# The latent attention's low rotated keys held in two zero-filled tiles of 128 rows

## The chip, the cores and the metric
One core of one Trainium2 chip runs the whole program. The metric is device time in microseconds (us) from launch to end. The kernel before takes 2837.29 us (median of 3 runs, 2834.54 to 2839.94).

## The reference, cut to what matters
The program is two transformer blocks on 512 tokens of width 1024: gated linear attention and a feed-forward layer, then multi-head latent attention (MLA) and a feed-forward layer, then a second block with convolution and expert lookup. The change lies in the MLA scores alone:

```
q_nope (8 heads x 128), q_rope (8 heads x 64);  k_nope (8 heads x 128), k_rope (64, one for all heads)
q_rope, k_rope = apply_rope(q_rope), apply_rope(k_rope)
s = (q_nope . k_nope  +  q_rope . k_rope) * 192 ** -0.5
p = softmax(where(key <= query, s, -inf));  o = p @ v
```

Everything is float32 in the reference.

## The kernel before
A tensor that enters a large product is kept as two parts in the fp32r format, a high part (the rounded value) and a low part (what rounding left). `split` (L240) makes them: ScalarE (ACT) copies the high part, VectorE (DVE) subtracts it for the low part. A product of two such tensors is three matmuls, high by high, high by low, low by high; `mm3` issues them at L274, L275 and L276. Weights arrive in units of 1 MB (`raw`, two buffers, issued from SyncE's queue, SP, at L267), and each unit is split the same way into `whi` and `wlo`. The engines run in parallel and meet at semaphores; each engine takes its instructions in one fixed order that a planner sets when the program is built.

The MLA stage runs in this order. Projections give the latents; the key's rotary part `pa`, `pb` is rotated on DVE into `kr` (L841 to L845). `kr` holds the same 64 rotated rows twice, on partitions 0 to 63 and 64 to 127. L846 and L847 split it into `krh` and `krl` (both named kr in the profile), each of 128 rows. The values `vn` follow (L857 to L861), and then the loop over 8 heads.

- `queries(h)`: for every second head it projects and rotates the queries of two heads (L872 to L876) and makes for each a tile `qs` (L880 on ACT, L881 on GpSimd, POOL). For an even head the tile has the high rotated query on rows 0 to 63 and the low one on rows 64 to 127; for an odd head it is the other way round. For every head it then projects and splits `kn` and `qn` (L240).
- `weigh(h)`: for each of four query blocks `qb`, with n = 128, 256, 384 and 512 keys, five matmuls add into one PSUM bank (L899 to L903). L900 takes all 128 rows of `qx` against `krh`, which gives high by high plus low by high at once. L901 takes only the 64 rows `rr` that hold the high query, against the same 64 rows of `krl`. Then DVE adds the mask (L904), finds the row maximum (L906, L907), ACT takes the exponential (L909), and DVE normalises (L910, L911).
- `attend(h)`: TensorE (PE) transposes the weights (L922), DVE copies them out (L924), PE multiplies by `vn` (L926), and ACT and DVE split the result into `hh` and `hl` (L928, L929).

The loop is written as weigh(h+1), attend(h), queries(h+2), and the planner interleaves them on PE. PSUM has eight banks, four with the tag "mm" and four with "acc". After the heads come the output projection, and further feed-forward and projection stages built on `mm3`.

The pool `mn` has a tag "araw" with two buffers of 128 x 1024. It streams the adaptive-norm weights through SP's queue at L319 for DVE's dot products at L312, in other stages than this one.

Of the kernel before, what the change touches and what calls it, by code (L numbers as in the profile page):

```python
# [10 lines left out]
F32 = mybir.dt.float32  # L11
F32R = mybir.dt.float32r
# [9 lines left out]
P = 128  # L22
S = 512
D = 1024
# [37 lines left out]
ARAW = 2  # L62
# [131 lines left out]
def block_kernel(ctx, tc, x_in, cs_in, wst, vec, cst, gmask, smask, pos, ada1, ada2, wgate, keys, ust, uex, vex, out):  # L194
    nc = tc.nc
    V, A_, T_, G_, SP = nc.vector, nc.scalar, nc.tensor, nc.gpsimd, nc.sync
# [7 lines left out]
    mn = main.enter_context(tc.tile_pool(name="mn", bufs=1))  # L204
    dr = ctx.enter_context(tc.tile_pool(name="dr", bufs=1, space=DRAM))

    def bank(tag="mm"):
        return ps.tile([P, S], F32, tag=tag, bufs=4, name=tag)
# [30 lines left out]
    def split(hi, lo, src, eng=None):  # L239
        state["split"] = (A_.copy(hi, src), (eng or V).tensor_sub(lo, src, hi.bitcast(F32)))  # L240
# [313 lines left out]
    with tc.tile_pool(name="gla", bufs=1, reuse_waits="tile") as gp:  # L554
# [24 lines left out]
        def gates():  # L579

            az, mz = [], []
            for h in range(GLA_H):
                z = bank("acc")
                T_.matmul(z, wg[:, h * P:(h + 1) * P], glr, start=True, stop=True)
                bg = vc("gla_b_gate", h)
                a = gp.tile([P, S], F32, tag="b", bufs=4, name="az")
                m = gp.tile([P, S], F32, tag="vn", bufs=8, name="mz")
                A_.activation(a, z, AF.Abs, bias=bg)
                V.tensor_scalar(m, z, bg, 0.0, op0=ALU.add, op1=ALU.min)
                az.append(a)  # L590
                mz.append(m)
            for a in az:
                e = A_.activation(a, a, AF.Exp, scale=-1.0)
            with tc.issue_after(e.ins):
                for h in range(GLA_H):
                    n = A_.activation(az[h], az[h], AF.Ln, bias=1.0)
                    V.tensor_sub(mz[h], mz[h], az[h])
                    V.tensor_tensor_scan(az[h], smk, mz[h], 0.0, op0=ALU.mult, op1=ALU.add)
            return az, n
# [102 lines left out]
        bs, n = gates()  # L702
        for what in GLA_ORDER.split():
            kind, h = what[0], int(what[1])
# [105 lines left out]
    with tc.tile_pool(name="mla", bufs=1, reuse_waits="tile") as mp:  # L810
# [13 lines left out]
        def latent_norm(ns, sq, gname, tag):  # L824
            rs = bcast(sq.rsqrt(tag))
            for i, n in enumerate(ns):
                V.scalar_tensor_tensor(cq[n], cq[n], vc(gname, i), rs, op0=ALU.mult, op1=ALU.mult)
                ch[n] = mp.tile([P, S], F32R, name=f"ch{n}")
                cl[n] = mp.tile([P, S], F32R, name=f"cl{n}")
                split(ch[n], cl[n], cq[n])  # L830
# [9 lines left out]
        kr = mp.tile([P, S], F32, tag="qr", bufs=1, name="kr")  # L840
        V.tensor_mul(kr, pa, cosT)  # L841
        pb = proj("mla_w_in", hh, hl)
        t = mn.tile([P, S], F32, tag="tmp", bufs=2, name="tmp")
        V.tensor_mul(t, pb, sinT)
        V.tensor_add(kr, kr, t)  # L845
        krh, krl = [mp.tile([P, S], F32R, name=f"kr{i}") for i in range(2)]  # L846
        split(krh, krl, kr)  # L847
        latent_norm((0, 1, 2), sqq, "mla_g_q", "n")
        cqh, cql = [ch[n] for n in range(3)], [cl[n] for n in range(3)]
        vn = [mp.tile([P, 1024], F32, name=f"mv{c}") for c in range(NT)]  # L850
# [38 lines left out]
        def weigh(h):  # L889

            kn, qn = kq.pop(h)
            qx = qrot.pop(h)
            rr = slice(h % 2 * 64, h % 2 * 64 + 64)
            prs = []
            for qb in range(NT):
                n = (qb + 1) * P
                qs = slice(qb * P, (qb + 1) * P)
                sc = bank("mm")
                T_.matmul(sc[:, :n], qn[0][:, qs], kn[0][:, :n], start=True, stop=False)  # L899
                T_.matmul(sc[:, :n], qx[:, qs], krh[:, :n], start=False, stop=False)  # L900
                T_.matmul(sc[:, :n], qx[rr, qs], krl[rr, :n], start=False, stop=False)  # L901
                T_.matmul(sc[:, :n], qn[1][:, qs], kn[0][:, :n], start=False, stop=False)
                T_.matmul(sc[:, :n], qn[0][:, qs], kn[1][:, :n], start=False, stop=True)  # L903
                V.tensor_add(sc[:, qs], sc[:, qs], cm)  # L904
                mx = mp.tile([P, 4], F32, tag="mx", bufs=4, name="mx")
                V.reduce_max(mx[:, 0:1], sc[:, :n], axis=mybir.AxisListType.X)  # L906
                V.tensor_scalar(mx[:, 1:2], mx[:, 0:1], -scale, None, op0=ALU.mult)  # L907
                pr = mp.tile([P, n], F32, tag=f"pr{qb}", bufs=2, name="pr")
                A_.activation(pr, sc[:, :n], AF.Exp, bias=mx[:, 1:2], scale=scale, accum_out=mx[:, 2:3])  # L909
                V.reciprocal(mx[:, 3:4], mx[:, 2:3])  # L910
                V.tensor_scalar(pr, pr, mx[:, 3:4], None, op0=ALU.mult)  # L911
                prs.append(pr)
            return prs
# [17 lines left out]
        prs = {}  # L931
        queries(0)
        prs[0] = weigh(0)
        queries(1)
        for h in range(MLA_H):
            if h + 1 < MLA_H:
                prs[h + 1] = weigh(h + 1)
            attend(h, prs.pop(h))
            if h + 2 < MLA_H:
                queries(h + 2)  # L940
# [31 lines left out]
    with tc.tile_pool(name="b2", bufs=1, reuse_waits="tile") as bp:  # L972
# [4 lines left out]
        for n in range(4):  # L977
            p = proj("w_in_2", hh, hl)
            t = bp.tile([P, WIDE], F32, tag=f"glu{n}", name="glu")[:, :PADC + S]
# [4 lines left out]
        for n in range(4):  # L984
            p = proj("w_in_2", hh, hl)
            t = mn.tile([P, S], F32, tag="tmp", bufs=2, name="tmp")
# [57 lines left out]
        for n in range(16):  # L1044
            p = proj("w_in_2", hh, hl)
            t = bp.tile([P, S], F32, name=f"sg{n}")
# [9 lines left out]
        for g in range(4):  # L1056
# [3 lines left out]
            t = mn.tile([P, S], F32, tag="tmp", bufs=2, name="tmp")  # L1060
# [15 lines left out]
        for n in range(4):  # L1076
            V.scalar_tensor_tensor(yc[n], yc[n], vc("conv_ln_g_2", n), rs, op0=ALU.mult, op1=ALU.mult)
            t = mn.tile([P, S], F32, tag="tmp", bufs=2, name="tmp")
# [19 lines left out]
    with tc.tile_pool(name="peer", bufs=1, reuse_waits="tile") as pp:  # L1098
# [38 lines left out]
        with tc.tile_pool(name="sel", bufs=1, reuse_waits="tile") as sp:  # L1137
# [179 lines left out]
            for h in range(PH):  # L1317
                qq, ql = [], []
                for half in range(2):
                    p = proj("w_query_2", hh, hl)  # L1320
                    t = sp.tile([P, 3 * P], F32, tag="q", bufs=4, name="q")
# [28 lines left out]
        with tc.tile_pool(name="exp", bufs=1, reuse_waits="tile") as ep:  # L1350
# [81 lines left out]
            for g in range(P // GJ):  # L1432
# [13 lines left out]
                for half in range(2):  # L1446
                    acc = [bank("acc") for _ in range(4)]
                    for j4 in range(GJ // 4):
# [3 lines left out]
                        for j in range(4):  # L1452
                            for dd in range(4):
                                o = j * 512 + dd * P
                                i = j4 * 4 + j
# [3 lines left out]
                    for dd in range(4):  # L1459
                        n = half * 4 + dd  # L1460
# [95 lines left out]
```

## Time and profile before

| | |
|---|---|
| Median of 3 runs | 2837.29 us |
| Profiled execution | 2844.19 us |
| Its span, first to last instruction | 2842.3 us |
| Mean granted TensorE clock | 0.981 of full speed |
| PE busy | 2716.3 us, 96% |
| DVE busy | 2109.8 us, 74% |
| ACT busy | 1070.5 us, 38% |
| POOL busy | 704.0 us, 25% |
| MLA head loop | from about 760 to 866 us in the span |

A row of a timeline gives the start in the span, the duration, the engine, the line, the operation, and the output and inputs; idle time before it stands in square brackets with what ended it. PEld is PE's weight load, which can run beside the matmul before it. Matmul ends are modelled, so the distance from one start to the next is the firmer number.

### The profile page before, as it was taken

The page shows a single profiled execution, that of the slowest core. Times are in us where ns is not written, and L with a number is a line of the kernel's source. Part 1 is how long each engine was busy: PE and PEld are TensorE (multiplying, and loading weights), DVE is VectorE, ACT ScalarE, POOL GpSimd, SP SyncE. Part 2 cuts the span into 40 slices and gives each one's busy share as a digit, 9 for nine tenths or more (in the row PEclk, how much of TensorE's full clock was granted, in tenths as well). Part 3 has the DMA queues.
Part 4 walks back from the last instruction along what each step waited for, and adds up shares of the span by engine and source line. Part 5 has one row for each costly group of instructions (what it writes and reads, how often), then busy time and mean ns, then how long its engine had stood idle before and what let it go on. Part 6 is the DMA issues. An engine that isn't in the chain of part 4 may idle for free. (4 is left out here: it accounts for less than half of the span.)

```text
span 2842.3 us, 38989 instructions
## 1 busy us (share of the span) xinstructions
PE 2716.3 (96%) x14889; PEld 2441.4 (86%) x14889; DVE 2109.8 (74%) x4011; ACT 1070.5 (38%) x1530; POOL 704.0 (25%) x556
## 2 busy tenths in 40 slices
PE   6789998999999999999999999998899999999998
PEld 4677887888778878888888889998899999999998
DVE  8874766435776774337966798888989898988986
ACT  4443322222433322233453336653333333333332
POOL 4541100001011000001521420003545455444550
PEclk9899999999999999999999999999999999999999
DMA  6441477422211674232223236656999998998993
GB/s 267 139 137 62 148 259 256 142 95 88 75 45 60 210 264 148 89 104 76 89 89 104 77 120 214 210 196 241 337 340 359 355 340 328 341 344 320 350 344 131
DMA packets 184363, 560.62 MB, mean 197 GB/s; under 512 B 13248, under 2 KB 66912, under 8 KB 157680
## 3 DMA queue, kind: packets, MB, share of 16 engines
q1 hardware_dynamic: 142352, 407.08, 40.9%
q0 software_dynamic: 41472, 151.01, 14.3%
q8 instruction: 117, 1.92, 0.3%
q14 instruction: 70, 0.57, 0.1%
q10 hardware_dynamic: 352, 0.03, 0.0%
HBM read 527.32 MB, written 30.75 MB: 196 GB/s over the span
## 5 line engine op out<-in xcount | busy, mean ns | idle before, releaser
L240 ACT CAST whi<-raw 128x1024 fp32r<-128x1024 f32 x510 | 535.6, 1051 | 1171.4 <-PE mm L275 689.7
L275 PE MATMUL mm<-hl,whi 128*128 128x512 f32 (+2 forms) x2544 | 899.8, 355 | 8.9 <-DVE hl L426 8.1
L274 PE MATMUL mm<-hh,whi 128*128 128x512 f32 (+2 forms) x2544 | 899.7, 355 | 2.7 <-ACT hh L425 2.0
L276 PE MATMUL mm<-hh,wlo 128*128 128x512 f32 (+2 forms) x2544 | 898.8, 354 | 0.1
L240 DVE TENSOR_TENSOR wlo<-raw,whi 128x1024 fp32r<-128x1024 f32 x472 | 580.2, 1230 | 296.8 <-ACT whi L240 288.0
L275 PEld LDWEIGHTS mm<-hl,whi 128*128 128x128 f32 x2544 | 482.4, 190 | 57.4 <-DVE hl L426 9.8
L274 PEld LDWEIGHTS mm<-hh,whi 128*128 128x128 f32 x2544 | 482.5, 190 | 49.5 <-ACT hh L425 2.6
L276 PEld LDWEIGHTS mm<-hh,wlo 128*128 128x128 f32 x2544 | 482.8, 190 | 48.2 <-issue 1.5
L240 POOL TENSOR_TENSOR wlo<-raw,whi 128x1024 fp32r<-128x1024 f32 x38 | 90.7, 2391 | 908.7 <-ACT whi L240 864.0
L1377 POOL DMA_INDIRECT rows<-vex,eidx x144 | 215.2, 1494 | 214.4 <-DVE y L1391 198.1
L1377 POOL DMA_INDIRECT rows<-uex,eidx x144 | 210.1, 1459 | 214.2 <-DVE rows L1381 164.9
L312 DVE SCALAR_TENSOR_TENSOR araw<-araw,sc 128x1024 f32<-128x1024 f32 x128 | 160.6, 1258 | 98.0 <-DMA araw<-ada 97.4
L1391 DVE SCALAR_TENSOR_TENSOR y<-rows,act,y 128x1024 f32<-128x1024 f32 x142 | 181.7, 1280 | 7.3 <-DMA rows<-vex,eidx 6.7
L1381 DVE SCALAR_TENSOR_TENSOR rows<-rows,hn 128x1024 f32<-128x1024 f32 x144 | 170.1, 1220 | 14.8 <-DMA rows<-uex,eidx 14.8
L274 PE MATMUL mm<-fh,whi 128*128 128x512 f32 (+1 forms) x396 | 147.5, 372 | 11.3 <-ACT fh L240 11.3
L275 PE MATMUL mm<-fl,whi 128*128 128x512 f32 (+1 forms) x396 | 147.7, 373 | 1.7 <-DVE fl L240 1.7
L276 PE MATMUL mm<-fh,wlo 128*128 128x512 f32 (+1 forms) x396 | 146.9, 371 | 0.0
L1310 ACT ACTIVATE stage<-acc 128x512 f32<-128x512 f32 x92 | 91.6, 1105 | 37.0 <-PE acc L1307 26.6
L1307 PE MATMUL acc<-oa,ob 128*128 128x128 f16 x736 | 101.5, 296 | 0.3 <-DVE oa L1298 0.2
L274 PEld LDWEIGHTS mm<-fh,whi 128*128 128x128 f32 x396 | 76.2, 192 | 24.6 <-ACT fh L240 12.1
L448 DVE SCALAR_TENSOR_TENSOR x<-mm,mod,x 128x512 f32<-128x512 f32 (+1 forms) x66 | 43.9, 666 | 62.8 <-PE mm L276 62.7
L275 PEld LDWEIGHTS mm<-fl,whi 128*128 128x128 f32 x396 | 76.1, 192 | 15.3 <-DVE fl L240 2.7
(1381 smaller groups left out, 4593.9 us busy)
## 6 DMA issues: line engine op xcount, KB each, us to landing
raw<-wst SPq DMA_DIRECT2D x127, 1024.0 KB, 4.9
araw<-ada SPq DMA_DIRECT2D x128, 512.0 KB, 4.6
raw<-ust SPq DMA_DIRECT2D x64, 1024.0 KB, 6.4
raw<-vex SPq DMA_DIRECT2D x64, 1024.0 KB, 7.6
gd<-stage SPq DMA_DIRECT2D x23, 1024.0 KB, 4.5
gt<-gd SPq DMA_DIRECT2D x16, 1472.0 KB, 9.4
aw<-ada SPq DMA_DIRECT2D x16, 512.0 KB, 8.9
spilled<-a SPq DMA_DIRECT2D x24, 184.0 KB, 3.1
```

The costliest lines, as they stand in the source:

```text
L240: state["split"] = (A_.copy(hi, src), (eng or V).tensor_sub(lo, src, hi.bitcast(F32)))
L274: T_.matmul(out_, wh, ah, start=first, stop=False)
L275: T_.matmul(out_, wh, al, start=False, stop=False)
L276: state["mm"] = T_.matmul(out_, wl, ah, start=False, stop=last)
L312: op(out=w, in0=w, scalar=1.0, in1=sc, op0=ALU.mult, op1=ALU.mult, accum_out=out_)
L448: V.scalar_tensor_tensor(x[n][:, cs], p[:, cs], gate[:, n:n + 1], x[n][:, cs], op0=ALU.mult, op1=ALU.add)
L1307: T_.matmul(p[:, t * P:(t + 1) * P], ob[:, q, :, t], oa[i][:, q, :, t], start=i == 0, stop=i == 1)
L1310: A_.mul(st[:, :, t1:t1 + 4].rearrange("p j t -> p t j"), p.rearrange("p (t j) -> p t j", t=4), 1.0 / GSC)
L1377: G_.indirect_dma_start(out=r, out_offset=None, in_=uex if up_ else vex, in_offset=bass.IndirectOffsetOnAxis(ap=eidx[:, n:n + 1] if n < P ...
L1381: V.scalar_tensor_tensor(r, r, 1.0, hn if n < P else hx, op0=ALU.mult, op1=ALU.mult, accum_out=act[:, n:n + 1])
L1391: V.scalar_tensor_tensor(z, r, act[:, n:n + 1], z, op0=ALU.mult, op1=ALU.add)
```

## The change
`krh` stays as it was. `krl` becomes the two halves of one tile `kz` of 128 x 1024 from the tag "araw". The first half holds the low key on rows 0 to 63 and zeros on rows 64 to 127, the second half the other way round. Two POOL memsets write the zeros, and two DVE subtractions on 64 rows each take the place of one on 128 rows. In `weigh`, the third matmul takes all 128 rows of `qx` against the half that belongs to the head's parity; the rows with the low query meet zeros.

```
-        krh, krl = [mp.tile([P, S], F32R, name=f"kr{i}") for i in range(2)]
-        split(krh, krl, kr)
+        krh = mp.tile([P, S], F32R, name="krh")
+        A_.copy(krh, kr)
+        kz = mn.tile([P, D], F32R, tag="araw", bufs=ARAW, name="kz")
+        krl = kz[:, :S], kz[:, S:]
+        for i, t in enumerate(krl):
+            on, off = slice(i * 64, i * 64 + 64), slice(64 - i * 64, 128 - i * 64)
+            G_.memset(t[off].bitcast(F32), 0.0)
+            V.tensor_sub(t[on], kr[on], krh[on].bitcast(F32))
...
-            rr = slice(h % 2 * 64, h % 2 * 64 + 64)
...
-                T_.matmul(sc[:, :n], qx[rr, qs], krl[rr, :n], start=False, stop=False)
+                T_.matmul(sc[:, :n], qx[:, qs], krl[h % 2][:, :n], start=False, stop=False)
```

## Rows read from the trace of the kernel before

**Rows 1.** The page's busy time, share and count of each engine, and its line of PE's busy tenths in 40 equal slices of the span.
```profile
PE 2716.3 (96%) x14889; PEld 2441.4 (86%) x14889; DVE 2109.8 (74%) x4011; ACT 1070.5 (38%) x1530; POOL 704.0 (25%) x556
PE   6789998999999999999999999998899999999998
```

**Rows 2.** Busy time by stretch: the head loop and a stretch of the expert stage, the longest. Columns: stretch, its length, then busy us (and instructions) of PE, PEld, DVE, ACT and POOL, granted clock, DMA share, GB/s.
```profile
760.00:866.00 106.00, 102.00 (x519) 78.88 (x518) 77.33 (x218) 42.75 (x98) 12.17 (x8) 0.97 0.12 40
...
2100.00:2200.00 100.00, 100.00 (x602) 100.00 (x601) 91.57 (x141) 37.99 (x54) 52.31 (x36) 1.00 0.96 353
```

**Rows 3.** Who waited for whom from 780 to 866 us: total us, times, longest us.
```profile
PEld acc L926 <- DVE pT L924: 4.5, 6, 0.7
...
PEld mm L901 <- issue: 2.9, 9, 0.4
PEld mm L902 <- issue: 2.6, 12, 0.2
PE acc L926 <- DVE pT L924: 2.3, 6, 0.4
```

**Rows 4.** PE's timeline in `weigh(4)`: the first matmul, the groups of 384 and 512 keys, and the transpose that follows.
```profile
819.36 0.33 PE L899 MATMUL mm<-kn,qn 128*128 128x128 f32 x1
...
821.31 0.34 PE L899 MATMUL mm<-kn,qn 128*128 128x384 f32 x1
821.48 0.34 PE L900 MATMUL mm<-kr,qs 128*128 128x384 f32 x1
821.75 0.44 PE L901 MATMUL mm<-kr,qs 64*128 64x384 f32 x1
822.12 0.44 PE L902 MATMUL mm<-kn,qn 128*128 128x384 f32 x1
822.39 0.34 PE L903 MATMUL mm<-kn,qn 128*128 128x384 f32 x1
822.57 0.39 PE L899 MATMUL mm<-kn,qn 128*128 128x512 f32 x1
822.80 0.40 PE L900 MATMUL mm<-kr,qs 128*128 128x512 f32 x1
823.13 0.49 PE L901 MATMUL mm<-kr,qs 64*128 64x512 f32 x1
823.55 0.50 PE L902 MATMUL mm<-kn,qn 128*128 128x512 f32 x1
823.88 0.39 PE L903 MATMUL mm<-kn,qn 128*128 128x512 f32 x1
824.12 1.03 PE L922 MATMUL acc<-ct,pr 128*128 128x128 f32 x8
```

**Rows 5.** PE's weight loads for three of those matmuls of 512 keys.
```profile
822.57 0.19 PEld L900 LDWEIGHTS mm<-kr,qs 128*128 128x128 f32 x1
823.12 0.18 PEld L901 LDWEIGHTS mm<-kr,qs 64*128 64x128 f32 x1 [0.36 <-issue]
823.55 0.19 PEld L902 LDWEIGHTS mm<-kn,qn 128*128 128x128 f32 x1 [0.24 <-issue]
```

**Rows 6.** PE's timeline: 14 matmuls of 128 columns in a row, and the start of the next.
```profile
827.29 1.72 PE L926 MATMUL acc<-pT,mv 128*128 128x128 f32 x14
828.77 0.48 PE L276 MATMUL mm<-ch,wlo 128*128 128x512 f32 x1
```

**Rows 7.** PE's timeline after `weigh(1)`: the start of `attend(0)`'s last products.
```profile
782.63 1.05 PE L926 MATMUL acc<-pT,mv 128*128 128x128 f32 x8
```

**Rows 8.** DVE's timeline after `weigh(1)`: the mask of the last score, and the copy that the products of rows 7 read; last, the first masks of `weigh(4)`.
```profile
779.77 0.30 DVE L904 TENSOR_TENSOR mm<-mm,ct 128x128 f32<-128x128 f32 x1 [0.60 <-PE mm L903]
...
781.31 0.68 DVE L924 COPY pT<-acc 128x512 f32<-128x512 f32 x1
...
821.22 0.59 DVE L904 TENSOR_TENSOR mm<-mm,ct 128x128 f32<-128x128 f32 x2 [1.08 <-PE mm L903]
```

**Rows 9.** PE's timeline at head 0: the first matmul of `weigh(0)`, and the first after its last.
```profile
762.11 0.33 PE L899 MATMUL mm<-kn,qn 128*128 128x128 f32 x1 [1.19 <-ACT qn L240]
...
769.54 0.63 PE L274 MATMUL mm<-ch,whi 128*128 128x512 f32 x1
```

**Rows 10.** Two stretches around the end of `weigh(0)`, with the columns of rows 2; the granted clock is the third number from the end.
```profile
764.00:769.50 5.50, 5.50 (x14) 3.49 (x14) 2.23 (x9) 1.69 (x6) 0.00 (x0) 0.50 0.22 91
...
770.50:771.00 0.50, 0.50 (x4) 0.40 (x3) 0.50 (x4) 0.00 (x0) 0.00 (x0) 1.00 0.00 0
```

**Rows 11.** DVE's timeline: the subtraction that makes `krl`, and the next idle time on DVE.
```profile
745.90 0.68 DVE L240 TENSOR_TENSOR kr<-kr,kr 128x512 fp32r<-128x512 f32 x1
...
748.71 1.23 DVE L240 TENSOR_TENSOR wlo<-raw,whi 128x1024 fp32r<-128x1024 f32 x1 [0.86 <-ACT whi L240]
```

**Rows 12.** POOL's timeline: its first work in the MLA stage, with the idle time before it.
```profile
760.46 3.06 POOL L881 TENSOR_TENSOR qs<-qr,qs 64x512 fp32r<-64x512 f32 x2 [63.25 <-ACT qs L880]
```

**Rows 13.** POOL's memsets of 128 x 512 in an earlier stage: count, then busy us, mean ns of one, idle us before.
```profile
L615 POOL MEMSET at<- 128x512 f32 x4 | 2.0, 529 | 1.1 <-DVE az L598 1.1
```

**Rows 14.** The buffers "araw": DVE's dot products from 100 to 760 us, with the least, median and largest duration in ns and the first and last start.
```profile
L312 DVE SCALAR_TENSOR_TENSOR araw<-araw,sc x76: 1202/1225/1672, 104.2 to 505.4; 128x1024 f32<-128x1024 f32 x76
```

**Rows 15.** SP's timeline: the first loads into "araw" after those.
```profile
940.16 1.47 SPq L319 DMA_DIRECT2D araw<-ada  x2
```

**Rows 16.** All matmuls of L901, with the columns of rows 14.
```profile
L901 PE MATMUL mm<-kr,qs x32: 322/434/792, 762.5 to 864.4; 64*128 64x128 f32 x8, 64*128 64x256 f32 x8, 64*128 64x384 f32 x8, 64*128 64x512 f32 x8
```

## The prediction
> **What bounds the kernel now.** I read the page first. PE is busy 96% of the span, and in 40 slices it falls under 80% only in the first two [rows 1]. The windows say the same by stage: PE 102.00 of 106 us in the head loop, where DVE has 77.33, and 100.00 of 100 us in the expert stage [rows 2]. So what shortens PE's stream should shorten the span, unless another engine is close behind. The waits of the head loop come third. PE waits for DVE's copies of the transposed probabilities for 2.3 us in six waits, and its weight loads stand before L901 and L902 with "issue" for 2.9 and 2.6 us, that is for nothing that the trace can name [rows 3]. The timeline of one `weigh` then shows what that is.
>
> **The step from full to half rows.** For 512 keys, L899 to L900 takes 0.23 us from start to start, L900 to L901 takes 0.33, L901 to L902 0.42, L902 to L903 0.33, and the next comes 0.24 after [rows 4]. The undisturbed step of these shapes is 0.23, so the 64-row product costs 0.10 before it, 0.19 after it and 0.10 one step later: 0.39 us. For 384 keys the steps are 0.17, 0.27, 0.37, 0.27 and 0.18: 0.10, 0.20 and 0.10 over 0.17 [rows 4]. The extra doesn't grow with the columns; it is a price per change of row count. The weight loads show how it arises. L900's load starts 0.23 us ahead of its matmul, under L899. L901's and L902's start only with their own matmuls, after PEld stood idle for 0.36 and 0.24 us [rows 4, 5]. Each group changes from 128 rows to 64 and back once, and there are 32 groups [rows 16].
>
> **What a `weigh` costs after.** The groups of 128 and 256 keys are interleaved: ten matmuls from 819.36 to 821.31, 1.95 us. Matmuls of 128 columns in a row start every 1.48/14 = 0.106 us [rows 6], and 256 columns come to half of 0.23, 0.115. The ten would take 0.53 + 0.58 = 1.11 us, 0.84 less. The 384 keys, now 1.26 us, would take 5 x 0.17 = 0.85, 0.41 less; the 512 keys, now 1.55, 5 x 0.23 = 1.15, 0.40 less [rows 4]. That is 1.65 us per head. I take 1.6, since the first step of the block, behind transposes in another format, may keep its 0.06.
>
> **What of it reaches the end, head by head.** Even heads 2, 4 and 6: in `weigh(4)` DVE stands idle for 1.08 us ahead of the first masks [rows 8], so it can start with the earlier scores, and I take all of it: 3 x 1.6 = 4.8 us. Odd heads: DVE follows closely. After `weigh(1)` PE starts products at 782.63 [rows 7] that read a copy done at 781.31 + 0.68 = 781.99, and DVE, in order, had only 0.60 us idle ahead of the last score [rows 8]. PE would be there at 781.03, the copy at the earliest at 781.39. So a new wait of some 0.36 us is late next, and 1.24 of 1.6 us are kept: heads 1, 3, 5 and 7 give 5.0 us.
>
> Head 0 runs at half clock. It starts after an idle 1.19 us, and the granted clock is 0.50 (1.2 GHz) from 764 on and back at 1.00 (2.4 GHz) at 770.5 [rows 9, 10]. If the clock returns at the same moment as now, work pulled into that stretch runs at half speed, and of the 2.0 us or so that the block shortens there about half is given back: 1.0 us. The sum is 4.8 + 5.0 + 1.0 = **10.8 us**. Its ends: all 32 groups at 0.40 and head 0 whole give 13.4 at the most, and if DVE follows no faster the least is nothing.
>
> **The preparation.** One DVE subtraction becomes two. On 64 rows I price each like the 128-row one, 0.68 us, since it has as many elements per row. DVE has 0.86 us idle 2 us later, waiting for ACT, and takes it up there [rows 11]; without that cover it would be 0.68 us once. The two memsets cost at most 0.53 us each, the time of 128 rows [rows 13], on a POOL idle for 63 us ahead of its first work here [rows 12]; without that cover they cost about 1 us once, ahead of the first `qs`. The tile takes one of two "araw" buffers. The last dot before started at 505.4 [rows 14], the next loads are issued at 940.16 [rows 15], and the last reader of the low key starts at 864.4 [rows 16], so neither side waits: 75 us of cover. Were it gone, SP would stand at the load with the 1 MB weight units queued behind it, and PE would wait for those. PE's third matmul streams as many columns on 128 rows as on 64, so it adds nothing by itself; its weight load takes 0.19 us against 0.18 [rows 5].
>
> **The time.** The profiled execution took 2844.19 us, so I expect 2833.4 for one like it. It lies 6.9 us above the median of the runs, 2837.29, and the same sum puts the median at **2826.5 us**. A measurement of this kernel tells about 0.2% from no change, 5.7 us: faster means under 2831.6.
>
> **The rivals.**
> - *DVE takes over.* If PE gains only what DVE has idle ahead of the last score, 0.60 us for each of 8 heads, as after `weigh(1)` [rows 8], the sum is 4.8 us and the median 2832.5, within 0.2%. For it speaks the order on DVE, where the copies stand behind the scores; against it DVE's 77 of 106 us, which become 77 of 95 [rows 2]. Chance 0.12.
> - *The load, not the row count.* The exposed 0.10 us steps could belong to loads that can't run under a matmul on the same rows, and filling the rows would then leave them so. Only one of the four tenths per group, the excess of the way back, would go: 32 x 0.10 = 3.2 us, median 2834.1. Against it: L900's load runs under L899's matmul, both on 128 rows [rows 4, 5]. Chance 0.07, with every other way in which the change does nothing, then 2837. The Trainium skill, in "TensorE: Matmul & The Clock Gate", Part 3, says that weight loads overlap matmuls in flight only where the row groups differ, which speaks against filling the rows; by that rule alone the sum would be 3.2 us and not 10.8. The trace disagrees with it as far as it goes, by that load's 0.23 us of lead.
> - *Slower: the clock falls.* At head 0 an idle 1.19 us stands ahead of 764 to 769.5 at half clock [rows 9, 10], some 6.6 us with its edges, which cost 3.3 us. With less work in each `weigh` and new waits, the same could befall the later heads. The price is 7 x 3.3 = 23 us, net 12.3 slower, median 2850. It decides from the fifth such fall on: 5 x 3.3 = 16.5, 5.7 above the gain. Against it: six waits on DVE's copies are there already, 0.4 us the longest [rows 3], and the head loop's mean clock of 0.97 leaves room for little more than head 0's fall [rows 2]. Chance 0.06.
>
> **How the numbers follow.** The forecast has 0.75; a small part of it, where the waits at odd heads are twice as long and head 0 gives nothing, falls short of 5.7 us, about 0.02. So faster has 0.73, within 0.2% 0.02 + 0.12 + 0.07 = 0.21, and slower 0.06. The range goes down to the largest sum, 2823.9, less half the 5.4 us spread of the runs, 2821.2; it goes up past the second rival and the case without effect, to 2837.5. Left out are the clock's falls and the tails.
>
> **What would show it.** In the changed trace, L901 has 128 rows and its load leads its matmul by about 0.2 us; the "issue" waits at L901 and L902 are gone; the five steps of 512 keys are all about 0.23 us, and a `weigh` takes about 3.2 us where 4.76 stood. DVE's idle ahead of L904 shrinks, and PE's waits for L924 grow by some 0.4 us in odd heads. The head loop ends about 10.8 us earlier, and every later stage keeps that distance. It is wrong if the steps around L901 stay at 0.33 and 0.42, if the distance shrinks again after the heads, or if the granted clock falls there.

## The result, and the profile after

| | before | after |
|---|---|---|
| Median of 8 runs each | 2835.91 us | 2823.81 us |
| Profiled execution | 2844.19 us | 2822.58 us |
| Its span | 2842.3 us | 2820.8 us |
| Mean granted TensorE clock | 0.981 | 0.985 |
| Head loop | 103.3 us | 90.5 us |

The ratio of the runs is 0.9949, with a 95% interval of 0.9935 to 0.9963: 14.5 us less, 10.5 to 18.4 (the two medians lie 12.1 us apart). "Head loop" is here the stretch from the first matmul of `weigh(0)` to the first one after `weigh(7)`: 762.11 to 865.40 before and 756.90 to 847.38 after.

In the kernel after, the lines of the loop stand five lower: L904 to L908 are the five matmuls that were L899 to L903, L909 is the mask, L927, L929 and L931 are the transpose, its copy and the product with `vn`. The page first; its rows answer to [rows 1].

```profile
PE 2700.4 (96%) x14889; PEld 2434.6 (86%) x14889; DVE 2104.2 (75%) x4012; ACT 1065.1 (38%) x1530; POOL 712.8 (25%) x558
PE   6789999999999999999999999998899999999998
```

PE has the same 14889 matmuls and 15.9 us less of busy time. The shares have not moved, and the 40 slices look alike: the page alone would not show where the time went. The windows do, with the columns of [rows 2]: the head loop, and in it the block of `weigh(0)`.

```profile
756.90:847.40 90.50, 87.40 (x509) 74.15 (x510) 73.53 (x213) 39.63 (x93) 10.55 (x8) 1.00 0.14 47
757.00:760.30 3.30, 3.30 (x20) 3.05 (x21) 2.74 (x10) 2.03 (x5) 1.27 (x1) 1.00 0.75 290
```

The head loop is 12.8 us shorter. Its granted clock is 1.00 where it was 0.97, and head 0, which stood at 0.50 [rows 10], runs at 1.00. The waits of the loop, 775 to 848 us, answer to [rows 3]: total us, times, longest us.

```profile
PE acc L931 <- DVE pT L929: 2.3, 6, 0.4
...
PEld mm L907 <- DVE qn L240: 1.2, 3, 0.4
```

The "issue" waits of PEld before the third and the fourth matmul, 5.5 us, are gone. PE's waits for the copies of the transposed weights are as before, 2.3 us in this window and 2.7 over the whole loop. DVE waits less for the scores: 10.8 us over the loop before, 2.1 after. New is a wait ahead of L907 in odd heads. PE's timeline, cut to three places: `weigh(0)` and the first matmul behind it (as [rows 9]), the middle of `weigh(1)` and the products after it (as [rows 7]), and `weigh(4)` (as [rows 4]).

```profile
756.90 0.33 PE L904 MATMUL mm<-kn,qn 128*128 128x128 f32 x1 [1.19 <-ACT qn L240]
...
760.34 0.40 PE L274 MATMUL mm<-ch,whi 128*128 128x512 f32 x1
...
766.29 0.34 PE L905 MATMUL mm<-krh,qs 128*128 128x384 f32 x1
766.69 0.33 PE L907 MATMUL mm<-kn,qn 128*128 128x128 f32 x1
...
768.94 1.28 PE L931 MATMUL acc<-pT,mv 128*128 128x128 f32 x10
...
772.00 1.05 PE L931 MATMUL acc<-pT,mv 128*128 128x128 f32 x8
...
806.29 0.33 PE L904 MATMUL mm<-kn,qn 128*128 128x128 f32 x1
...
807.12 0.33 PE L907 MATMUL mm<-kn,qn 128*128 128x128 f32 x1
807.28 0.28 PE L908 MATMUL mm<-kn,qn 128*128 128x128 f32 x1
807.39 0.33 PE L907 MATMUL mm<-kn,qn 128*128 128x256 f32 x1
807.56 0.28 PE L908 MATMUL mm<-kn,qn 128*128 128x256 f32 x1
807.68 0.34 PE L904 MATMUL mm<-kn,qn 128*128 128x384 f32 x1
...
808.55 0.39 PE L904 MATMUL mm<-kn,qn 128*128 128x512 f32 x1
808.78 0.40 PE L905 MATMUL mm<-krh,qs 128*128 128x512 f32 x1
809.01 0.40 PE L906 MATMUL mm<-kz,qs 128*128 128x512 f32 x1
809.25 0.39 PE L907 MATMUL mm<-kn,qn 128*128 128x512 f32 x1
809.47 0.40 PE L908 MATMUL mm<-kn,qn 128*128 128x512 f32 x1
809.71 1.04 PE L927 MATMUL acc<-ct,pr 128*128 128x128 f32 x8
```

Read the starts. For 512 keys they now stand 0.23, 0.23, 0.24, 0.22 and 0.24 us apart, where [rows 4] had 0.23, 0.33, 0.42, 0.33 and 0.24. The block of `weigh(4)` takes 809.71 - 806.29 = 3.42 us where it took 4.76. PEld's timeline shows why, beside [rows 5]:

```profile
808.78 0.19 PEld L906 LDWEIGHTS mm<-kz,qs 128*128 128x128 f32 x1
809.01 0.19 PEld L907 LDWEIGHTS mm<-kn,qn 128*128 128x128 f32 x1
```

Each load starts with the matmul before its own, 0.23 or 0.24 us ahead of its own, and PEld has no idle time. The pair of traces adds up like this: the head loop gives 12.8 us; 1.9 come in the stage behind it; 5.2 lie ahead of the first matmul of `weigh(0)`, in stages that the change doesn't touch; and the rest, 1.6 of 21.5, comes later. The first matmul of `weigh(0)` started anywhere from 760.45 to 762.42 us in three other traces whose `weigh` is the kernel before's, from 759.2 to 762.4 in four with full rows in some heads only, and from 754.6 to 758.3 in two with full rows in all. One of the former, `e1_prep_only`, has the whole preparation in it. So the 5.2 us are at most partly the change's; the 8 runs of each give 10.5 to 18.4 us, which holds the loop's 12.8 and the 14.7 with the stage behind it, and not the 21.5 of this pair.

### The profile page after: what moved, and what is told of

It is laid out like the page before. It is cut to its first block, busy times and chain, and to the rows that moved or that the text cites. A ratio compares the mean times of both kernels' runs of the same rounds, so it can differ in the third digit from the quotient of the medians.

```text
span 2820.8 us, 38992 instructions
## 1 busy us (share of the span) xinstructions
PE 2700.4 (96%) x14889; PEld 2434.6 (86%) x14889; DVE 2104.2 (75%) x4012; ACT 1065.1 (38%) x1530; POOL 712.8 (25%) x558
## 5 line engine op out<-in xcount | busy, mean ns | idle before, releaser
L274 PE MATMUL mm<-hh,whi 128*128 128x512 f32 (+2 forms) x2544 | 897.4, 354 | 5.3 <-ACT hh L425 4.5
L274 PEld LDWEIGHTS mm<-hh,whi 128*128 128x128 f32 x2544 | 479.9, 189 | 52.7 <-ACT hh L425 5.7
L274 PE MATMUL mm<-fh,whi 128*128 128x512 f32 (+1 forms) x396 | 147.2, 372 | 10.1 <-ACT fh L240 10.1
L274 PEld LDWEIGHTS mm<-fh,whi 128*128 128x128 f32 x396 | 76.3, 193 | 23.3 <-ACT fh L240 11.0
```

Of the source, the lines that this page charges most:

```text
L274: T_.matmul(out_, wh, ah, start=first, stop=False)
```

## The experiments

Two theories stood against each other at first. **The change of row count:** PE pays each time that a 64-row matmul stands between 128-row ones. **The preparation or the load:** the time is saved by the order of the work before the loop, or by anything else that comes with the new tile. Later a third question came up, what happens at head 0. The ratio in the table sets the runs of a kernel against runs of the kernel before on the same chip. The loop and the blocks are read from one trace of each kernel; a block is a `weigh`, from its first matmul to the next one that follows it.

| run | loop us | block of head 0 | later blocks, even / odd | ratio to before (95%) |
|---|---|---|---|---|
| before | 103.3 | 7.43 | 4.76 / 4.76 | 1 |
| after | 90.5 | 3.44 | 3.42 / 3.62 | 0.9949 (0.9935 to 0.9963) |
| e1_prep_only | 103.4 | 7.24 | 4.76 / 4.76 | 0.9994 (0.9985 to 1.0004) |
| e2_no_zeros | 90.5 | 3.44 | 3.42 / 3.62 | 0.9953 (0.9936 to 0.9969) |
| e3_grouped | 96.2 | 4.75 (1.08 of it a wait) | 3.60 / 4.2 | 0.9973 (0.9961 to 0.9986) |
| e4_two_changes | 133.5 | 8.34 | 6.26 to 8.98 | 1.0121 (1.0102 to 1.0140) |
| e5_head0_wide | 99.0 | 3.43 | 4.76 / 4.76 | 0.9988 (0.9974 to 1.0001) |
| e6_others_wide | 91.8 | 4.75 | 3.42 / 3.61 | 0.9968 (0.9953 to 0.9984) |
| e7_twin | 110.3 | 8.13 | 4.91 to 7.09 | 1.0020 (1.0009 to 1.0031) |

**e1_prep_only.** The changed kernel with the old 64-row product; the zeros, the split subtraction and the "araw" buffer stay.

```
-                T_.matmul(sc[:, :n], qx[:, qs], krl[h % 2][:, :n], ...)
+                T_.matmul(sc[:, :n], qx[rr, qs], krl[h % 2][rr, :n], ...)
```

> Edit: the preparation of the changed kernel alone (zero-filled tiles, two POOL memsets, two DVE subtractions, one buffer of araw), while the third product still takes 64 rows of it. Theory (the change of row count on PE is the price): nothing is gained, within 3 us of before; the steps around the third product stay at 0.33, 0.42 and 0.33 us for 512 keys. Rival (the preparation, the moved buffer or the planner's new order brings the gain): 10 to 15 us faster than before, with those steps unchanged. If the preparation costs something, it is 0.7 us slower or less.

It stands at 2839.92 us beside 2840.15, and the blocks stay at 4.76 us. The preparation alone gains and costs nothing that can be measured. On DVE, the two subtractions took 1.38 us in a row here too, and nothing waited for them.

**e2_no_zeros.** The kernel before with the full rows alone, without zeros.

```
-                T_.matmul(sc[:, :n], qx[rr, qs], krl[rr, :n], ...)
+                T_.matmul(sc[:, :n], qx[:, qs], krl[:, :n], ...)
```

> Edit: the kernel before, its preparation untouched, and only the third product widened to all 128 rows of the low key that is already there twice (it adds low query by low key, which the zeros of the changed kernel leave out). Theory: the same gain as the changed kernel, 12 to 14 us, steps of 0.23 us for 512 keys, no wait in it that the changed kernel lacks. Rival (the preparation matters): less than half of that gain.

2826.24 beside 2840.15 us, with a loop and blocks like those of the kernel after to 0.04 us. The row count by itself gives the whole gain.

**e3_grouped.** The four 64-row products of a `weigh` stay, but stand in a row behind the sixteen full ones: one change there and back per head instead of four.

```
-                T_.matmul(sc[:, :n], qx[rr, qs], krl[rr, :n], start=False, stop=False)
...
+            for qb, sc in enumerate(scs):
+                T_.matmul(sc[:, :n], qx[rr, qb * P:n], krl[rr, :n], start=False, stop=True)
```

> Edit: the kernel before with 64-row products, but the four of a head issued one after the other behind the other 16 matmuls, so that the row count changes once there and back per head and not four times. Theory (a price per change of row count, 0.4 us): 8 x 0.4 = 3.2 us of the price are left, so 8 to 10 us faster than before, less what later scores cost in new waits; between the 64-row products the steps are as for full rows, 0.11 to 0.23 us. Rival (a price of each 64-row product, 0.4 us): no gain, and 0.33 to 0.42 us between these products.

PE's timeline at the end of a block, on 64 rows and off them again:

```profile
832.31 0.39 PE L903 MATMUL mm<-kn,qn 128*128 128x512 f32 x1
832.63 0.90 PE L908 MATMUL mm<-kr,qs 64*128 64x128 f32 x4
833.46 0.71 PE L934 MATMUL acc<-pT,mv 128*128 128x128 f32 x4
```

The first 64-row product comes 0.32 us after L903, not 0.23, and the four take 0.83 us, where full rows would step by 0.11, 0.11, 0.17 and 0.23, together 0.62. That is 0.21 + 0.09 = 0.30 us more, and the next fourteen products, up to 835.04, take 0.10 more than in [rows 6]. So four in a row pay about once what one pays alone. Even blocks go from 4.76 to 3.60 us, which is 1.16 of the 1.34 us that full rows save; odd ones hold three or four matmuls of `attend` as well, about 0.5 to 0.6 us, and without those come to 3.65. The kernel is 7.6 us faster in the median (4.0 to 11.1), just under the 8 to 10 expected. Without those matmuls and without a new wait in head 0 the eight blocks are some 11.7 us shorter than before, the loop only 7.1. In head 0 PE now waits 1.08 us ahead of L274, for ACT's exponential of a score (L917), since all four scores end together. After heads 2, 4 and 6 the load for L274 waits for the same, about 0.35 us each. Where the rest, some 2 us, went I did not trace.

**e4_two_changes.** The product on 64 rows is cut into two halves of the keys, one ahead of L902 and one behind it: two changes per group.

```
-                T_.matmul(sc[:, :n], qx[rr, qs], krl[rr, :n], ...)
+                T_.matmul(sc[:, :n // 2], qx[rr, qs], krl[rr, :n // 2], ...)
                 T_.matmul(sc[:, :n], qn[1][:, qs], kn[0][:, :n], ...)
+                T_.matmul(sc[:, n // 2:n], qx[rr, qs], krl[rr, n // 2:n], ...)
```

> Edit: the kernel before with the 64-row product of each group cut into two of half the columns, with a full-row product between them, so that the row count changes twice there and back per group and no column is added. Theory (0.4 us per change there and back): 32 x 0.4 = 12.8 us more on PE, 10 to 14 us slower than before. Rival (the price is a share of the columns streamed on 64 rows): within 3 us of before, since the columns are the same.

Dearer by 33.1 us, and the loop by 30.2, over twice the 32 x 0.39 = 12.5 us of the price per change, and far above the 10 to 14 expected. The window of the loop and PE's timeline of 512 keys, first at the full clock and then at half, tell the two parts apart.

```profile
757.90:891.50 133.60, 130.73 (x541) 97.28 (x542) 77.99 (x217) 41.89 (x97) 10.58 (x8) 0.82 0.09 32
```

```profile
776.42 0.39 PE L899 MATMUL mm<-kn,qn 128*128 128x512 f32 x1
776.65 0.40 PE L900 MATMUL mm<-kr,qs 128*128 128x512 f32 x1
776.98 0.38 PE L901 MATMUL mm<-kr,qs 64*128 64x256 f32 x1
777.29 0.50 PE L902 MATMUL mm<-kn,qn 128*128 128x512 f32 x1
777.72 0.38 PE L903 MATMUL mm<-kr,qs 64*128 64x256 f32 x1
778.03 0.50 PE L904 MATMUL mm<-kn,qn 128*128 128x512 f32 x1
778.37 1.27 PE L927 MATMUL acc<-pT,mv 128*128 128x128 f32 x10
...
850.39 0.63 PE L899 MATMUL mm<-kn,qn 128*128 128x512 f32 x1
...
853.71 2.33 PE L927 MATMUL acc<-pT,mv 128*128 128x128 f32 x10
```

At the full clock the group takes 778.37 - 776.42 = 1.95 us where [rows 4] has 1.55: 0.40 for one more change, as the theory has it. But the loop's granted clock is 0.82, and the same group later takes 3.32 us at 1.2 GHz, 1.70 times as long. Such falls to the lower level come in seven of the eight heads (not in head 1, from which the first group is); before, there was one, in head 0. If time doubled at half clock, (1 - 0.82) x 133.6 = 24 us of the loop would be lost to that, where (1 - 0.97) x 103.3 = 3 were. But the group takes 1.70 times as long and not twice, so I estimate 48 x (1 - 1/1.70) = 20 us for the 48 us at half clock. Less the 3 of before and with the 12.5 of the changes, that is near the 30.2. PE did not wait more than before: 2.7 us for DVE's copies and the 1.19 us ahead of head 0, in this trace as in the others. It changed its row count more often.

**e7_twin.** The same two halves one after the other: as many instructions as in `e4_two_changes`, but one change per group.

> Edit: the kernel before with the 64-row product of each group cut into two of half the columns that follow each other, with nothing between them; the row count changes once there and back per group as before, and there is one 64-row product more. Theory: within 4 us of before (a floor of 0.06 to 0.11 us for the shortest ones at the most, 32 x 0.05 = 1.6 us). Rival (each 64-row product costs 0.4 us): 12 us slower or more, as with the full-row product between the halves.

```profile
809.64 0.40 PE L899 MATMUL mm<-kn,qn 128*128 128x512 f32 x1
...
810.20 0.38 PE L901 MATMUL mm<-kr,qs 64*128 64x256 f32 x1
810.42 0.28 PE L902 MATMUL mm<-kr,qs 64*128 64x256 f32 x1
810.63 0.50 PE L903 MATMUL mm<-kn,qn 128*128 128x512 f32 x1
810.97 0.40 PE L904 MATMUL mm<-kn,qn 128*128 128x512 f32 x1
811.20 1.06 PE L927 MATMUL acc<-pT,mv 128*128 128x128 f32 x8
```

PE's timeline in `weigh(3)`: 1.56 us for 512 keys, as before with one product. The second half costs nothing beyond its columns. The run is still 6.6 us slower (2.6 to 8.8 by its interval), more than the 4 expected. Its blocks are 4.91 us (0.15 more) where the order is kept, in the odd heads. In the even heads the planner put full-row products between the two halves of one group, which makes a fifth change: 5.23 us in heads 2 and 6, and in heads 0 and 4 the clock fell, 8.13 and 7.09 us. It parts instructions from changes within a group, and is no clean measure of the whole.

**e5_head0_wide** and **e6_others_wide.** Full rows in head 0 alone, and in all heads but 0.

```
-            rr = slice(h % 2 * 64, h % 2 * 64 + 64)
+            rr = slice(h % 2 * 64, h % 2 * 64 + 64) if h else slice(0, P)     # e5
+            rr = slice(0, P) if h else slice(0, 64)                           # e6
```

> Edit: the kernel before, with the third product on all 128 rows of the low key in head 0 alone (which there adds low query by low key); heads 1 to 7 keep 64 rows. Theory (the changes of row count behind the idle 1.19 us bring the clock down at head 0): the granted clock stays at 1.00 there, head 0's block takes about 3.4 us in place of 7.4, and the kernel is some 4 us faster than before. Rival (whether the clock falls there is a matter of chance in each execution): the block may still run at half clock, and without a fall only 1.6 us are gained.

> Edit: the reverse; heads 1 to 7 take all 128 rows (with low query by low key added), head 0 keeps its 64-row products. Theory: head 0 still falls to half clock and its block takes about 7.4 us, the other heads save 1.2 to 1.4 us each, so 8 to 9 us faster than before. Rival (chance): head 0's block at full clock, about 4.8 us, and 11 us or more faster.

Head 0 alone takes the loop from 103.3 to 99.0 us, 4.3 less, and the median 3.2 less (7.4 less to 0.3 more). Its block is at the full clock. All but head 0 give 9.2 us in the median, and in that profile head 0, with its four products on 64 rows, did not fall either. That one trace stood against four, so more traces followed: of the kernel before, and then two of this kernel and one each of the kernels after and before.

> Edit: none, the kernel before once more, for a second trace. Theory: head 0 at half clock again, its block 7.4 us. Rival (chance): full clock there, 4.8 us.

> Edit: none against the kernel with 64 rows in head 0 alone, once more, for a second trace of head 0. Theory (the changes of row count bring the clock down at head 0, but not in every execution): about 7 us for head 0's block. Rival (with the other heads wide the clock never falls there): 4.75 us again.

> Edit: as the run before it, a third trace. Theory: about 7 us for head 0's block in at least one of the two. Rival: 4.75 us in both.

> Edit: none, the changed kernel once more. Theory: head 0's block at full clock, 3.4 us, and the head loop 90.5 us long, as in its first trace. Rival (chance): head 0 at half clock, about 6 us, and the loop 93 us.

> Edit: none, the kernel before, a third trace. Theory: head 0's block between 6 and 7.5 us and the head loop 103 us. Rival (chance): 4.8 us and 100.6 us.

PE's timeline of head 0's block, of `e6_others_wide` and then of `e9_others_wide_again`, the same program:

```profile
762.38 0.33 PE L899 MATMUL mm<-kn,qn 128*128 128x128 f32 x1 [1.19 <-ACT qn L240]
...
767.13 0.40 PE L274 MATMUL mm<-ch,whi 128*128 128x512 f32 x1
```

```profile
761.22 0.33 PE L899 MATMUL mm<-kn,qn 128*128 128x128 f32 x1 [1.19 <-ACT qn L240]
...
767.50 0.63 PE L274 MATMUL mm<-ch,whi 128*128 128x512 f32 x1
```

4.75 us at the full clock, and 6.28 with a fall; the third trace has 7.39. The kernel before took 7.43, 6.39 and 7.39, the kernel after 3.44 and 3.45. (The single times of these traces, 2840.06 for e8 and 2832.76, 2830.00, 2820.88 and 2846.91 for e9 to e12, with 2833.51 for another run of the kernel before beside them, differ too much among equal kernels to be read for a few us; the blocks are what they are for.) Over all traces with 64-row products in each group of head 0 (before three times, e1, e4, e6, e7, e9, e10) the clock fell there in 8 of 9. Over those with full rows or a single change in head 0 (after twice, e2, e3, e5) it fell in none of 5. The idle 1.19 us ahead of the block [rows 9] stands in all of them. So that wait alone does not bring the fall; with the changes of row count behind it, it is likely and not certain. What in the changes does it is not shown: in e3 head 0 has as many columns on 64 rows as before and no fall, but that is one trace.

## Why the prediction was right, and where its terms were off

**The mechanism held.** The price is paid per change of row count. It goes when the rows are filled, with zeros or without (e2); it stays with the preparation alone (e1); it shrinks when four products share one change (e3); and it grows by 0.40 us per group of 512 keys with a second change (e4). The prediction took it as the same for all columns. In `weigh(4)` it is 0.39 us for 384 and for 512, and 0.56 for the groups of 128 and 256 together, about 0.28 each. The Trainium skill's page "TensorEngine Tiling (Array Packing)", section "Key Properties", says that a change of tiling mode drains TensorE. The traces agree as far as they show it: the loads across a change start only with their own matmul, and for 384 and 512 columns the price is 0.4 us there and back at 2.4 GHz. The rule of the Trainium skill's page "TensorE: Matmul & The Clock Gate", Part 3, which the prediction names beside the rival about the load, that a weight load overlaps a matmul in flight only where the row groups differ, does not hold as put: on the same 128 rows each load leads its matmul by 0.23 us, and the saving per group of 512 keys is 0.40 us and not 0.10.

**The sum came out near by errors that cancel in part, so the total is in part luck.** 10.8 us were predicted and 12.8 measured in the loop, with 1.9 more behind it in the profiled pair. By term:

- *Even heads, 4.8 us: 4.0.* A block takes 3.42 us, not the 3.2 of the prediction, and 3 x 1.34 = 4.0. The groups of 384 and 512 keys take 0.87 and 1.16, as worked out. The ten short matmuls take 807.68 - 806.29 = 1.39 us where I had 1.11, so they save 0.56 us and not 0.84. My 0.106 us per step came from a run of 14 matmuls of one line [rows 6]; here the step behind L907 is 0.16 for 128 columns and 0.17 for 256, and the one behind L908 0.11 and 0.12. I have not found why. The nearer rows were in the block itself: before, among full rows, the steps behind L902 were 0.17 as well, and I should have taken those. PE's timeline of the kernel before, the last four of the ten:

```profile
820.74 0.33 PE L902 MATMUL mm<-kn,qn 128*128 128x128 f32 x1
820.91 0.27 PE L903 MATMUL mm<-kn,qn 128*128 128x128 f32 x1
821.02 0.33 PE L902 MATMUL mm<-kn,qn 128*128 128x256 f32 x1
821.19 0.28 PE L903 MATMUL mm<-kn,qn 128*128 128x256 f32 x1
```

- *Odd heads, 5.0 us: 4.6.* 4 x 1.15, close, but by another wait. I expected PE to wait 0.36 us for the copy ahead of the last products. That did not come: the products at 772.00 start 3.06 us after the block's end at 768.94, and before they started as far behind it, at 782.63 after 779.57. What came is a wait within the block: L907 reads the low part of the queries, and DVE makes that one late. DVE's timeline:

```profile
743.72 1.23 DVE L240 TENSOR_TENSOR wlo<-raw,whi 128x1024 fp32r<-128x1024 f32 x1
...
765.95 0.68 DVE L240 TENSOR_TENSOR qn<-mm,qn 128x512 fp32r<-128x512 f32 x1
...
770.72 0.68 DVE L929 COPY pT<-acc 128x512 f32<-128x512 f32 x1
```

  `qn` ends at 766.63, L907 starts at 766.69, and the step from L905 is 0.40 us. The copy ended at 771.40, 0.60 us ahead of the products. It moved with the block, since DVE's wait for the last score, 0.60 us before [rows 8], is gone as well. I had looked at the next consumer behind the block, and not at what the block's own inputs still had in hand.
- *Head 0, 1.0 us: 4.0.* This term was mis-sized. 7.43 to 3.44 us: about 1.3 is the change of row count, as e6 has it at the full clock (4.75 to 3.44), and 2.7 is the clock (7.43 to 4.75). I took the fall to lower clock for given, as a thing that the idle 1.19 us had brought about; the runs tie it to the changes of row count in the block.
- *Behind the heads, 0: about 1.3.* From the loop's end to the load of an ACT table at L739 it took 75.3 us before and 73.4 after. It took 74.3 to 75.7 in the seven other traces with 64-row products in heads 1 to 7, and 73.4 to 73.9 in the five others with full rows there. The difference is a fall of the clock at L369, in the stage behind the heads. L369 on PE's timeline, with the idle time ahead of it, and a window from there (columns of [rows 2]), of the kernel before and then of `e11_after_again`:

```profile
916.99 0.66 PE L369 MATMUL acc<-ct,ry 128*128 128x128 f32 x2 [2.23 <-DVE ry L357]
...
917.00:920.50 3.50, 3.50 (x17) 3.50 (x18) 2.99 (x8) 1.15 (x3) 0.00 (x0) 0.53 0.00 0
```

```profile
896.76 0.40 PE L369 MATMUL acc<-ct,ry 128*128 128x128 f32 x2 [2.23 <-DVE ry L357]
...
896.80:900.30 3.50, 3.50 (x28) 3.35 (x29) 3.15 (x9) 2.57 (x5) 0.54 (x1) 1.00 0.00 0
```

  A granted clock of 0.53 over 3.5 us costs (1 - 0.53) x 3.5 = 1.6 us at most. The wait is not the change's: all traces have it but one of the kernel after and `e6_others_wide`. The fall is another matter. Over the 3.5 us from L369 on the granted clock is 0.51 to 0.67 in all eight traces with 64-row products in heads 1 to 7, and 1.00 in all six with full rows there, four of which have the wait. So the fall goes with the narrow products, though the last of them lies some 50 us earlier. How it could come from them no run shows; this part stays open. The prediction had "every later stage keeps that distance".

4.0 + 4.0 + 4.6 = 12.6 of the loop's 12.8. With 1.3 behind it the sum is near 14, within what the runs gave, 10.5 to 18.4. The upper end of the predicted sum is itself 0.2 us too high: 28 x 0.40 + 2.0 is 13.2, not 13.4.

**The preparation at nothing: right.** The memsets ran at 500.5 us, where the planner put them on an idle POOL. DVE's two subtractions take 1.38 us, and the next `wlo`, at 743.72, starts without the idle 0.86 us that stood there before [rows 11].

**The rivals.** DVE does not take over: it is busy for 73.5 of 90.5 us, PE's waits for its copies stay at 2.7 us over the loop, and what comes new is the 0.2 us or so per odd head. The load rival falls with the steps of 0.23 us in the kernel after and in e2. The rival of the falling clock had a real mechanism and put it to the wrong cause: it expected new waits to bring falls, and set its price at 3.3 us each, where head 0's fall cost 2.7. The runs show falls that come with changes of row count, so that fewer changes meant fewer falls: the sign was the other way round. With the cause right, the term for head 0 would have been 3 to 4 us, and the forecast about 2823.5 to 2824.5.

## What to carry to other kernels

One narrow product between full ones costs twice: at its two borders, here 0.39 us for 384 and 512 columns and about 0.28 for 128 and 256, and in the clock. Look on PE's timeline for steps longer than those of the same columns at full rows and for loads that start only with their own matmul, and then fill the rows with whatever is at hand, or set narrow products side by side, which here gained less (ratio 0.9973 against 0.9949). When a stretch at half clock lies in what a change touches, ask what brought it about before taking it as given.

## What was not expected of the hardware

Changes of row count go along with a lower granted clock, without any more idle time on PE: 32 more of them took the mean over the loop from 0.97 to 0.82 (e4), while the loops with full rows stand at 1.00, and so does the one with a single change per head (e3). But the 28 in heads 1 to 7 leave the clock at 1.00 in the loop as long as each group has one (e5), so one change per group does not bring a fall by itself. In e7 the clock fell in two of the four heads with a fifth change, one of them head 0, and in none of the four without. At the lower level of 1.2 GHz the price of a change grows too: a group of 512 keys with two changes took 3.32 us against 1.95. Full rows of 512 step by 0.43 us there (769.54 to 769.97 in the trace of before), 2.15 for five, so about 0.58 us is left for each change, where it was 0.40. The fall in head 0 is not certain from one execution to the next: the same program took 4.75, 6.28 and 7.39 us for that block. And a fall some 50 us behind the last narrow product went with the narrow products too, in 8 of 8 traces against 0 of 6.
